# Rows of six tiles turned by VectorE in blocks of 32, and stored by blocks, in the out stage of a hybrid decoder layer

## The chip, the core and the metric

The kernel runs on one core of one Trainium2 chip. The metric is the device time of one execution in microseconds (us). The names of the engines are those of the profile: PE is TensorE (matrix products, and turns, which are products with an identity matrix), DVE is VectorE, ACT is ScalarE, POOL is GpSimd, and SP is the queue that issues nearly all DMAs.

## The reference, cut to what matters

One decoder layer on 2048 prompt tokens and 64 sample tokens, all in float32, width 1024:

```python
proj = einsum('btd,de->bte', rms_norm(x, g_mix_pre), w_in)
attn, gla_out = window_attention(proj), gated_linear_attention(proj)
mix = einsum('bte,ed->btd', concatenate([attn, gla_out], -1), w_out)
x = x + rms_norm(mix, g_mix_post)
h = rms_norm(x, g_ffn_pre)
u = relu(einsum('btd,df->btf', h, w_up))
f = einsum('btf,fd->btd', u * u, w_down)
return x + rms_norm(f, g_ffn_post), ...
```

The change lies between `mix` and `u`: the rows of `h` have to be turned, so that the 1024 columns lie along the partitions, before the product with `w_up` can be made.

## The kernel before

The tokens are 16 tiles of 128 prompt rows (0 to 15) and one tile of 64 sample rows (16). Each float32 product is made from parts: an operand is rounded to a high part (by ACT) and the rest, its low part (by DVE), and PE multiplies high by high, high by low and low by high.

**Stages.** The input projection and the attention of both kinds come first, then the out stage (about 635 to 849 us), then the up and down products in two halves of 1024 tokens each. In the first stages the code's order is kept by force on every engine (`InOrder`); tables like `G_FIRST_FILL` say how many steps of other work go between the steps of a tile. That table is for tile 0, whose queries are weighted with the decays into `XQ` by small DVE products, while PE makes the projection of the sample rows (`gproj`), which ACT and DVE fold from two halves of 64 rows into `gp_s`. In the out stage most instructions go to the engines directly (`nc.tensor`, `nc.vector`, `nc.scalar`), and the framework's scheduler sets each engine's order from the data dependencies, its own costs and the order of the code.

**The out stage.** It takes the tiles in the order `B_ORDER` = 0, 4, 1, 5, 2, 6, 3, 7, 16, 8, 12, 9, 13, 10, 14, 11, 15. Per tile i:

- The mixed operand `mt_i` is loaded (L1534) and parted: ACT makes the high part (L231), DVE the low part (L232), each in two instructions of 128x512. Two buffers alternate. Tile 15 has only half of it here.
- PE makes `out_i_0` and `out_i_1`, two halves of 512 columns in two banks, with 48 matmuls (L1581). Three in a row are high by high, high by low and low by high, so the third is the first to read the low part. Two pairs of banks alternate between the tiles.
- ACT squares both halves (L1696); DVE adds the sums (L1697), and prepares the root (L219) that POOL takes (L221). DVE weights both halves with it into `x1_i` (L1703), which frees the banks, and adds the residual in `bx_i` (L1704), stored as `x1_d`.
- ACT squares `bx_i` (L1809), then follow L219, POOL's root and the second norm into `x1_i` (L1812).
- PE turns `x1_i` with eight 128x128 products (L1822) into `xnT_i_0` and `xnT_i_1`; ACT copies these into `ht` (L1831).

The code has the norms of a tile two tiles behind its product (`early`). The tiles of a half are taken in pairs j and j + 4 (8 and 12, 9 and 13, ...). `ht` holds seven planes of 4 x 128 tokens for the pair: planes 0 and 1 are the first tile's, 6 and 2 the second's, and four subtractions (L1840) make the others for a product scheme with seven in place of eight multiplications. For tiles 8 to 15 one buffer, `ht_8`, serves all pairs. The planes are stored in `h_d`, two by L1836 after the first tile of a pair and five by L1845 after the second, and the up products fetch them later (L1857, `fetch_h`) and part them (L1899 on ACT, L1900 on DVE, called from `load_h`). `uX` is the first of the up products, `sam` the sample's, and `xsT` the turned sample rows. Tile 11's copies and the last store wait for the up stage (`late_copies`, L2153). L143 is the line of the queue that keeps an order by hand; all that passes through it bears this line.

Of the kernel before, what the change touches and what calls it, by code (L numbers as in the profile page):

```python
# [12 lines left out]
F32 = mybir.dt.float32  # L13
# [3 lines left out]
ALU = mybir.AluOpType  # L17
# [57 lines left out]
G_ORDER = (0, 1, 2, 3)  # L75
G_FILL = (3, 5, 6, 10, 8, 2, 14, 4, 4, 10, 8, 20)
G_LAST_FILL = (2, 4, 5, 7, 6, 2, 11, 2, 3, 7, 6, 15)
G_FIRST_FILL = (6, 6, 6, 10, 10, 4, 16, 4, 4, 5, 5, 20)
S_WAIT = (2, 6)
WO_PARTS = ((), (0, 1, 2), (3, 4, 5), (6, 7))  # L80
B_ORDER = (*(j + b for j in range(4) for b in (0, 4)), NB, *(j + b for j in range(4) for b in (8, 12)))
# [72 lines left out]
def hybrid_step_kernel(ctx: ExitStack, tc: tile.TileContext, I, O):  # L154
# [24 lines left out]
    def bank(shape, kind, name):  # L179

        return ps.tile(shape, F32, tag=kind, name=name, bufs=1 if kind in "de" else 2)
# [9 lines left out]
    dpool = ctx.enter_context(tc.tile_pool(name="dpool", bufs=1, space=DRAM))  # L191
    mix_d = [dpool.tile([P, KT, rows(i)], F32, name=f"mix_d{i}") for i in range(NTILE)]
    xt_d = [dpool.tile([P, 2, KT, rows(i)], F32, name=f"xt_d{i}") for i in range(NTILE)]
    h_d = [dpool.tile([P, 7, KT // 2, BT], F32, name=f"h_d{sb}") for sb in range(NSB)]
    s_d = [[dpool.tile([P, 7, BT], F32, name=f"s_d{sb}_{fc}") for fc in range(NFC)] for sb in range(NSB)]
    t_d = [dpool.tile([P, 4, 512], F32, name=f"t_d{fc}") for fc in range(NFC)]
    wo_d = [dpool.tile([P, 2, D], F32, name=f"wo_d{k}") for k in range(KT - 1)]
# [1595 lines left out]

    late_copies, latest_store = [], []

    def residual(i, banks, tensor=nc.tensor, scalar=nc.scalar, vector=nc.vector):

        n = rows(i)
        x = res_x.pop(i, None) or load_x(i)[0]
        ssq = sp.tile([P, 48], F32, tag="ssq", name=f"bssq_{i}", bufs=2)  # L1800
        junk = sp.tile([P, D], mybir.dt.bfloat16, tag="junk", name=f"bjunk_{i}", bufs=1)
        x1 = R["x"].tile([P, D], F32, tag="x1", name=f"x1_{i}", bufs=2)
        if i == NB:
            banks = [folded(x1[:NS, c * 512 : (c + 1) * 512], p_) for c, p_ in enumerate(banks)]
        if banks:
            g = g_mix if tensor is nc.tensor else [gpost[:, c * 512 : (c + 1) * 512] for c in range(2)]
            yield from mixed(i, banks, x, x1, junk, ssq, g, sp, scalar, vector)
        rs = ssq[:, 3:5]
        scalar.activation(junk[:n], x[:n], AF.Square, accum_out=ssq[:n, 2:3])  # L1809
        yield  # L1810
        rsqrt_mean(sp, rs[:n, 1:2], ssq[:n, 2:3], n, D, vector=vector)
        vector.scalar_tensor_tensor(x1[:n], x[:n], rs[:n, 1:2], gpre[:n], op0=ALU.mult, op1=ALU.mult)  # L1812
        yield
        sb, j, second = i // 8, i % 4, i % 8 >= 4
        q = slice(j * P, (j + 1) * P)
        if i < NB and not second and i:
            sums[sb, j] = sums[sb, j - 1] if sb and j else ht_place(f"ht_{i}")
        for h in range(2):
            kk = slice(h * 4, h * 4 + 4)
            pt = (bank([P, 512], "ce"[h], f"xnT_{i}_{h}") if te is tensor else next_bank("cdce", f"xnT_{i}_{h}")).rearrange("p (k t) -> p k t", k=4)  # L1820
            for k in range(4):
                tensor.transpose(pt[:, k, :n], x1[:n, (h * 4 + k) * P : (h * 4 + k + 1) * P], ident[:n, :n])  # L1822
            if i == NB:
                split_copy(xsT[:, kk, :NS], xsT[:, kk, NS:], pt[:, :, :NS], vector)
                continue
            ht = sums[sb, j]
            copy = (ht[:, (6, 2)[h] if second else h], pt, AF.Copy)
            if i == B_ORDER[-2]:
                late_copies.append(copy)
            else:  # L1830
                scalar.activation(*copy)  # L1831
            if sb == 0 and not second:
                split_copy(H[h + 1][0][:, :, q], H[h + 1][1][:, :, q], pt, vector)
        if i == NB or not second:
            if i < NB and sb and i != B_ORDER[-2]:
                nc.sync.dma_start(h_d[sb][:, :2, :, q], ht[:, :2])  # L1836
            return
        yield
        for out, a, b in ((4, 6, 0), (6, 2, 6), (5, 2, 4), (3, 1, 5)):
            vector.tensor_tensor(ht[:, out], ht[:, a], ht[:, b], op=ALU.subtract)  # L1840
            if out == 6 and i == B_ORDER[-1]:
                yield
        if i == B_ORDER[-3]:
            yield
        latest_store[:] = [nc.sync.dma_start(h_d[sb][:, 2:, :, q], ht[:, 2:])]  # L1845

    h_raws = {}

    def fetch_h(sb, p, home="h"):
        h_raws[p] = []  # L1850
        for k in range(0, KT // 2, 2):
            if isinstance(home, tuple):
                pool, tag = U[home[k // 2]], "s"
            else:
                pool, tag = {"h": hs_pool, "t": keep}.get(home) or U[home], f"{home}{k // 2}"
            raw = pool.tile([P, 2, BT], F32, tag=tag, name=f"hraw_{sb}_{p}_{k}", bufs=1)
            fetched = nc.sync.dma_start(raw, h_d[sb][:, p - 1, k : k + 2])  # L1857
            h_raws[p].append(raw)
        return fetched

    def load_h(sb, p, scalar=nc.scalar, vector=nc.vector):
        h_place(sb, p)
        for n, raw in enumerate(h_raws.pop(p)):
            split_by(scalar, vector, *(t[:, 2 * n : 2 * n + 2] for t in H[p]), raw)
            yield 1.3

    def split_apart(sb, p):
# [52 lines left out]
    for n, i in enumerate(B_ORDER[2:]):  # L1920
        early.append((i, []))
        mixing = out_projecting(nc.tensor, i, early[-1][1])
        run(mixing, 24 if i == B_ORDER[-1] else 48)
        if n == 0:
            first_rows = residual(*early.pop(0))
            next(first_rows)
            second = residual(*early.pop(0))
            next(second)
            next(second)
            run(first_rows)  # L1930
        elif n == 1:
            run(second)
        if i == B_ORDER[-1]:
            waiting_rows = residual(*early.pop(0))
            run(waiting_rows, 5)
        elif n > 1:
            run(residual(*early.pop(0)))
        run(mixing)
        if n == len(B_ORDER) - 5:
            with tc.issue_after(loaded.ins):  # L1940
                first_up = load_up(0, 0)
            with tc.issue_after(first_up.ins):
                gpost = gains(I["g_mix_post"][0], 0, "gpost")
            split_up(0, 0, 0)
            split_up(0, 0, 1)
            fetch_h(0, 5)
# [201 lines left out]
    def opening(p, taken, ahead, add):  # L2148

        if p == 1:  # L2150
            for copy in late_copies:
                ac.activation(*copy)
            nc.sync.dma_start(h_d[1][:, :2, :, 3 * P :], sums[1, 3][:, :2])  # L2153
            taken(p)
            next(last_rows)
            loaded = placing[0]
            for n, raw in enumerate(h_raws[3]):
                with tc.issue_after(loaded.ins):
                    loaded = nc.sync.dma_start(raw, h_d[0][:, 2, 2 * n : 2 * n + 2])
            next(seventh)  # L2160
        elif p == 0:
            next(last_rows)
            sums_24(0, 0, dv)
        elif p == 2:
            taken(p)
            ahead("a")
        elif p == 8:
            taken(p)
            split_sums(0, 0, 24, ac, dv)
            run(load_h(0, 6, ac, dv))  # L2170
            U.pop("tmp").release()
        elif p == 5:
            taken(p)
            next(last_rows)
            next(last_rows)
            close_pools(R)
            for q in H_LATE[3:]:
                h_pools[q] = open_pool(f"h_{q}")
            ahead("s13")
            run(load_h(0, 3, ac, dv))  # L2180
            h_place(0, 4)
            loaded = None
            for k in range(0, KT // 2, 2):
                with tc.issue_after(loaded.ins) if loaded else nullcontext():
                    loaded = nc.sync.dma_start(f32(H[4][1][:, k : k + 2]), h_d[0][:, 3, k : k + 2])
            with tc.issue_after(loaded.ins):
                latest_store[:] = [load_up(0, 2)]
        elif p == 7:
            taken(p)
            split_in_place(4)  # L2190
        elif p == 9:
            taken(p)
            ahead("13")
            ahead("s24")
            run(last_rows)
        elif p == 6:
            next_X.append(bank([P, BT], "a", "uX_0_1"))
            up_product(0, 1, 1, next_X[0])
        elif p == 3:
            with tc.issue_after(latest_store[0].ins):  # L2200
                for half in range(2):
                    load_down(0, half)
        else:
            ahead("24")
            split_up(0, 1, 1, ac, None)
            taken(6)
            add(6, 1, "Z")
            split_low(0, 1, 1, dv)
            add(1, 1, "V")
# [420 lines left out]
```

## Time and profile before

| | |
|---|---|
| runs | 2138.22, 2137.28, 2135.93 us; median 2137.28 |
| profiled execution | 2138.09 us, span 2136.3 us |
| granted PE clock | 0.999 |
| busy | PE 99%, PE's weight loads 86%, DVE 72%, ACT 57%, POOL 10% of the span |
| out stage, PE | 48 matmuls of a tile from 777.82 to 788.84 us, the turn of a tile from 777.03 to 777.82 |

A timeline row begins with the start and the duration in us, then engine, line, operation, what it writes and reads, shapes and the count of equal instructions in a row; a bracket at the end gives the idle time before it and what ended it. The duration of a row reaches to the end of its last instruction, so rows of one engine can overlap by the depth of its pipeline; the distance between starts is what an instruction costs its engine.

### The profile page before, as it was taken

Reading aid. Unit: us, or ns where it says so; the run is one execution under the profiler, and the core shown is the slowest. Engines: PE = TensorE matmul, PEld = TensorE weight load, DVE = VectorE, ACT = ScalarE, POOL = GpSimd, SP = SyncE. Lnnn points to the kernel's source line nnn. Section 1 sums busy time; section 2 is a strip of 40 time slices with the busy share of each in tenths; the row PEclk is TensorE's granted clock in tenths of the full one; section 3 lists DMA queues with packets and bytes.
Section 4 is the critical chain, followed back from the end, with each engine's and each line's share of the span. In section 5 each row is a group of like instructions: output and inputs, shape, how many; then the busy total and the mean of one; then the engine's idle time right before and its main releaser. Section 6 shows DMA issues by size and latency. Waiting matters only on the chain.

```text
span 2136.3 us, 34547 instructions
## 1 busy us (share of the span) xinstructions
PE 2124.3 (99%) x11828; PEld 1839.5 (86%) x11828; DVE 1528.0 (72%) x3209; ACT 1209.9 (57%) x2690; POOL 223.0 (10%) x393
## 2 busy tenths in 40 slices
PE   9999999999999999999999999999999999999998
PEld 9999999999998888888888888888888888888887
DVE  7999878788886667888887655557766666555576
ACT  7999867566764445655554644344454444544454
POOL 4676510000001110000000000000000000000000
PEclk9999999999999999999999999999999999999999
DMA  7444334546667668687876777668544443766685
GB/s 244 150 148 142 113 100 93 128 113 166 189 201 265 202 208 269 223 274 260 277 257 230 262 236 223 209 197 281 185 149 158 157 158 134 253 204 197 190 273 179
DMA packets 309324, 421.73 MB, mean 197 GB/s; under 512 B 80204, under 2 KB 213308, under 8 KB 305036
## 3 DMA queue, kind: packets, MB, share of 16 engines
q1 hardware_dynamic: 308988, 419.26, 61.2%
q8 instruction: 93, 1.52, 0.3%
q14 instruction: 83, 0.68, 0.1%
q10 hardware_dynamic: 160, 0.27, 0.0%
HBM read 270.34 MB, written 148.57 MB: 196 GB/s over the span
## 4 chain that ended last, share of the span: by engine, by line
PE 95%; ACT 2%; DVE 2%; DMA 1%; issue 0%; POOL 0%; DVEq 0%; SPq 0%; ACTq 0%; POOLq 0%
PE dn L143 28%; PE gproj L143 12%; PE uc L143 8%; PE uX L143 8%; PE out L1581 7%; PE proj L143 6%; PE ud L143 4%; PE ue L143 4%; PE ub L143 4%; PE sam L143 2%; PE dsam L143 1%; PE sc L143 1%; PE pT L143 1%; PE av L143 1%; PE out L143 1%; PE xT L143 1%
## 5 line engine op out<-in xcount | busy, mean ns | idle before, releaser
L143 PE MATMUL dn<-o0t,o0s 128*128 128x512 f32 x888 | 345.5, 389 | 0.5 <-DVE f L2268 0.3
L143 PE MATMUL dn<-o0t,o1s 128*128 128x512 f32 x888 | 345.6, 389 | 0.0
L143 PE MATMUL dn<-o1t,o0s 128*128 128x512 f32 x888 | 345.6, 389 | 0.0
L2254 DVE TENSOR_TENSOR o1s<-rs,o0s 128x512 fp32r<-128x512 f32 x224 | 154.7, 691 | 223.3 <-ACT o0s L2253 221.0
L2253 ACT ACTIVATE o0s<-rs 128x512 fp32r<-128x512 f32 x224 | 141.1, 631 | 295.0 <-PE dn L143 261.5
L143 PE MATMUL gproj<-wg,gxh 128*128 128x384 f32 x1024 | 269.7, 341 | 0.0
L143 ACT ACTIVATE st<-st 128x512 f32<-128x512 f32 x224 | 141.1, 630 | 103.9 <-DVE st L143 99.0
L143 PEld LDWEIGHTS dn<-o0t,o0s 128*128 128x128 f32 x888 | 166.8, 188 | 37.2 <-DVE f L2268 1.1
L143 PEld LDWEIGHTS dn<-o1t,o0s 128*128 128x128 f32 x888 | 166.7, 188 | 35.1
L143 PEld LDWEIGHTS dn<-o0t,o1s 128*128 128x128 f32 x888 | 166.7, 188 | 35.0
L143 PE MATMUL gproj<-wg,gxl 128*128 128x384 f32 x576 | 186.4, 341 | 1.7 <-DVE gp_s L143 1.6
L143 PE MATMUL uc<-H,s 128*128 128x512 f32 x768 | 186.5, 391 | 0.0
L143 PEld LDWEIGHTS gproj<-wg,gxh 128*128 128x128 f32 x1024 | 184.3, 188 | 2.5 <-issue 2.1
L143 PE MATMUL uX<-H,w 128*128 128x512 f32 x768 | 185.2, 390 | 0.0
L143 PEld LDWEIGHTS uX<-H,w 128*128 128x128 f32 x768 | 144.0, 188 | 30.3
L143 PEld LDWEIGHTS uc<-H,s 128*128 128x128 f32 x768 | 143.0, 188 | 30.6 <-ACT st L143 0.2
L1581 PE MATMUL out<-wo,mt 128*128 128x512 f32 x680 | 158.8, 392 | 0.4 <-DVE x L1703 0.3
L2254 DVE TENSOR_TENSOR o1t<-rt,o0t 128x512 fp32r<-128x512 f32 x222 | 152.2, 686 | 4.2 <-ACT o0t L2253 4.1
L1581 PEld LDWEIGHTS out<-wo,mt 128*128 128x128 f32 x680 | 126.4, 188 | 27.0 <-issue 1.0
L2253 ACT ACTIVATE o0t<-rt 128x512 fp32r<-128x512 f32 x222 | 136.9, 618 | 9.0 <-DMA rt<-t_d 7.1
L221 POOL TENSOR_TENSOR frs<-rs_v,half 128x1 f32<-128x1 f32 (+1 forms) x13 | 11.5, 891 | 1197.8 <-DVE rs_v L219 1197.8
L143 DVE TENSOR_TENSOR st<-st 128x512 f32<-128x512 f32 x160 | 110.6, 691 | 29.5 <-ACT st L143 25.2
(451 smaller groups left out, 4238.8 us busy)
## 6 DMA issues: line engine op xcount, KB each, us to landing
s_d<-st SPq DMA_DIRECT2D x32, 1792.0 KB
rs<-s_d SPq DMA_DIRECT2D x224, 256.0 KB
raw<-in_w_up SPq DMA_DIRECT2D x64, 512.0 KB
rt<-t_d SPq DMA_DIRECT2D x128, 256.0 KB
rt<-in_w_down SPq DMA_DIRECT2D x96, 256.0 KB
t<-in_w_down SPq DMA_DIRECT2D x64, 256.0 KB
t_d<-t SPq DMA_DIRECT2D x32, 512.0 KB
h_d<-ht SPq DMA_DIRECT2D x8, 1280.0 KB
```

The lines of the kernel that those rows point to most:

```text
L143: ins = call(*a, **k)
L221: return nc.gpsimd.tensor_tensor(out, v[:n], e, op=ALU.pow)
L1581: te.matmul(banks[c], x, w[:, c * 512 : (c + 1) * 512], start=k + u == 0, stop=k == KT - 1 and u == n - 1,)
L2253: high = nc.scalar.activation(hi, raw, AF.Copy)
L2254: low = nc.vector.tensor_tensor(lo, raw, f32(hi), op=ALU.subtract)
```

## The change

Four parts. First, for the tiles 8, 12, 9, 13, 10 and 14 PE's turns and ACT's copies give way to two DVE transposes of 128x512 each, which turn every 32x32 block within itself; what the whole turn would do beyond that, moving blocks between groups of 32 partitions, is left to the stores. Tiles 11 and 15 keep PE's turns, and ACT's copies write the same layout by blocks. Second, `h_d[1]` is laid out by tile, block and plane; where one DMA of 128 partitions stored, four DMAs of 32 partitions do (`store_blocks`), the subtractions work on views of 128x4x128, the fetch has runs of 128 numbers, and ACT and DVE part it through a view. Third, two numbers of `G_FIRST_FILL` change, 10, 10 to 13, 7. Fourth, `run(first_rows)` is called four matmuls into the next tile.

```diff
-G_FIRST_FILL = (6, 6, 6, 10, 10, 4, 16, 4, 4, 5, 5, 20)
+G_FIRST_FILL = (6, 6, 6, 13, 7, 4, 16, 4, 4, 5, 5, 20)
...
-    h_d = [dpool.tile([P, 7, KT // 2, BT], F32, name=f"h_d{sb}") for sb in range(NSB)]
+    h_d = [dpool.tile(s, F32, name=f"h_d{sb}") for sb, s in enumerate(([P, 7, KT // 2, BT], [P, 4, 4, 7, P]))]
...
+    def by_blocks(ht):
+        return ht.rearrange("p u k t -> p (u k t)").rearrange("p (b u k x) -> p b u k x", b=4, u=7, k=4)
+
+    def store_blocks(j, us):
+
+        ht, dst = by_blocks(sums[1, j]), h_d[1][:, j]
+        if j == 3:
+            return nc.sync.dma_start(dst[:, :, us], ht[:, :, us].rearrange("p b u k x -> p b u (k x)"))
+        for c in range(4):
+            src = ht[c * 32 : c * 32 + 32, :, us].rearrange("t a u k x -> t a (u k x)")
+            stored = nc.sync.dma_start(dst[:, c, us].rearrange("(a t) u e -> t a (u e)", a=4), src)
+        return stored
...
+            u = (6, 2)[h] if second else h
+            if 8 <= i < NB and j < 3:
+                vector.transpose(
+                    by_blocks(sums[sb, j])[:, :, u].rearrange("t a k x -> t k a x"),
+                    x1[:, h * 512 : (h + 1) * 512].rearrange("x (k a t) -> x k a t", k=4, a=4),
+                )
+                continue
...
-            copy = (ht[:, (6, 2)[h] if second else h], pt, AF.Copy)
+            out = ht[:, u]
+            if sb:
+                out = by_blocks(ht)[:, :, u].rearrange("p c k x -> p k c x")
+                pt = pt.rearrange("p k (c x) -> p k c x", c=4)
+            copy = (out, pt, AF.Copy)
...
-                nc.sync.dma_start(h_d[sb][:, :2, :, q], ht[:, :2])
+                store_blocks(j, slice(2))
...
+        t = by_blocks(ht).rearrange("p b u k x -> p u b (k x)") if sb else ht
         for out, a, b in ((4, 6, 0), (6, 2, 6), (5, 2, 4), (3, 1, 5)):
-            vector.tensor_tensor(ht[:, out], ht[:, a], ht[:, b], op=ALU.subtract)
+            vector.tensor_tensor(t[:, out], t[:, a], t[:, b], op=ALU.subtract)
...
-        latest_store[:] = [nc.sync.dma_start(h_d[sb][:, 2:, :, q], ht[:, 2:])]
+        latest_store[:] = [store_blocks(j, slice(2, 7)) if sb else nc.sync.dma_start(h_d[0][:, 2:, :, q], ht[:, 2:])]
...
-            fetched = nc.sync.dma_start(raw, h_d[sb][:, p - 1, k : k + 2])
+            if sb:
+                raw = raw.rearrange("p b t -> p (b t)").rearrange("p (m e) -> p m e", e=P)
+            src = h_d[1][:, k : k + 2, :, p - 1].rearrange("p j c e -> p (j c) e") if sb else h_d[0][:, p - 1, k : k + 2]
+            fetched = nc.sync.dma_start(raw, src)
...
+        if n == 1:
+            run(mixing, 4)
+            run(first_rows)
         run(mixing, 24 if i == B_ORDER[-1] else 48)
...
-            run(first_rows)
```

The lines move: the second norm L1812 becomes L1825, ACT's second square L1809 becomes L1822, the subtractions L1840 become L1866, the stores L1836 and L1845 become L1806, the fetch L1857 becomes L1886, and the block transposes are L1835.

The scheduler also sets other instructions in another order. Three places are shown. The first is DVE's queue where tile 12's rows and the low part of `mt_13`, the operand of the product after next, are made. Before:

```order
L1703 SCALAR_TENSOR_TENSOR x1_12_10685<-out_12_0_10447,bssq_12_10683,wo0_3_9385 128x512
L1703 SCALAR_TENSOR_TENSOR x1_12_10685<-out_12_1_10472,bssq_12_10683,wo1_3_9386 128x512
L1704 TENSOR_TENSOR bx_12_10681<-x1_12_10685,bx_12_10681 128x1024
L232 TENSOR_TENSOR mt_13_10625<-mt_13_10625 128x512 x2
L219 TENSOR_SCALAR rs_v_10697<-bssq_12_10683 128x1
L1812 SCALAR_TENSOR_TENSOR x1_12_10685<-bx_12_10681,bssq_12_10683,gpre_9738 128x1024
L1697 TENSOR_TENSOR bssq_9_10776<-bssq_9_10776 128x1
```

After:

```order
L1703 SCALAR_TENSOR_TENSOR x1_12_10678<-out_12_0_10447,bssq_12_10676,wo0_3_9385 128x512
L1703 SCALAR_TENSOR_TENSOR x1_12_10678<-out_12_1_10472,bssq_12_10676,wo1_3_9386 128x512
L1704 TENSOR_TENSOR bx_12_10674<-x1_12_10678,bx_12_10674 128x1024
L219 TENSOR_SCALAR rs_v_10690<-bssq_12_10676 128x1
L1825 SCALAR_TENSOR_TENSOR x1_12_10678<-bx_12_10674,bssq_12_10676,gpre_9738 128x1024
L1835 STREAM_TRANSPOSE ht_8_10611<-x1_12_10678 128x4x4x32 x2
L1866 TENSOR_TENSOR ht_8_10611<-ht_8_10611 128x4x128 x4
L232 TENSOR_TENSOR mt_13_10618<-mt_13_10618 128x512 x2
L1697 TENSOR_TENSOR bssq_9_10762<-bssq_9_10762 128x1
```

The low part of `mt_13` (L232) moved from behind the residual sum (L1704) to behind the second norm, the two transposes and the four subtractions of tile 12.

The second is the end of out(13), on DVE and on ACT. The names `mt_10` and `mt_14` are the operands of the next two products. DVE before:

```order
L1704 TENSOR_TENSOR bx_9_10774<-x1_9_10778,bx_9_10774 128x1024
L232 TENSOR_TENSOR mt_10_10718<-mt_10_10718 128x512 x2
L219 TENSOR_SCALAR rs_v_10790<-bssq_9_10776 128x1
L1812 SCALAR_TENSOR_TENSOR x1_9_10778<-bx_9_10774,bssq_9_10776,gpre_9738 128x1024
L1697 TENSOR_TENSOR bssq_13_10865<-bssq_13_10865 128x1
L219 TENSOR_SCALAR rs_v_10871<-bssq_13_10865 128x1
L1703 SCALAR_TENSOR_TENSOR x1_13_10867<-out_13_0_10631,bssq_13_10865,wo0_3_9385 128x512
```

DVE after:

```order
L1835 STREAM_TRANSPOSE ht_8_10611<-x1_9_10764 128x4x4x32 x2
L1697 TENSOR_TENSOR bssq_13_10844<-bssq_13_10844 128x1
L219 TENSOR_SCALAR rs_v_10850<-bssq_13_10844 128x1
L1703 SCALAR_TENSOR_TENSOR x1_13_10846<-out_13_0_10624,bssq_13_10844,wo0_3_9385 128x512
L1703 SCALAR_TENSOR_TENSOR x1_13_10846<-out_13_1_10649,bssq_13_10844,wo1_3_9386 128x512
L232 TENSOR_TENSOR mt_10_10704<-mt_10_10704 128x512 x2
L232 TENSOR_TENSOR mt_14_10786<-mt_14_10786 128x512 x2
```

ACT before:

```order
L231 ACTIVATE mt_10_10718<-mt_10_10718 128x512 x2
L1809 ACTIVATE bjunk_9_10777,bssq_9_10776<-bx_9_10774 128x1024
L1696 ACTIVATE bjunk_13_10866,bssq_13_10865<-out_13_0_10631 128x512
L1696 ACTIVATE bjunk_13_10866,bssq_13_10865<-out_13_1_10656 128x512
L1831 ACTIVATE ht_8_10611<-xnT_12_0_10701 128x512
L1831 ACTIVATE ht_8_10611<-xnT_12_1_10707 128x512
L231 ACTIVATE mt_14_10807<-mt_14_10807 128x512 x2
```

ACT after:

```order
L1822 ACTIVATE bjunk_9_10763,bssq_9_10762<-bx_9_10760 128x1024
L1696 ACTIVATE bjunk_13_10845,bssq_13_10844<-out_13_0_10624 128x512
L1696 ACTIVATE bjunk_13_10845,bssq_13_10844<-out_13_1_10649 128x512
L231 ACTIVATE mt_10_10704<-mt_10_10704 128x512 x2
L231 ACTIVATE mt_14_10786<-mt_14_10786 128x512 x2
```

On DVE the low part of `mt_10` moved from behind tile 9's residual sum to behind tile 13's weighting of its product (L1703), and on ACT the high part from ahead of the squares of `out_13_0` and `out_13_1` (L1696) to behind them.

The third is the end of the stage. DVE, around the low part of `mt_15`, before:

```order
L1703 SCALAR_TENSOR_TENSOR x1_14_11041<-out_14_0_10813,bssq_14_11039,wo0_3_9385 128x512
L1840 TENSOR_TENSOR ht_8_10611<-ht_8_10611 128x512
L1703 SCALAR_TENSOR_TENSOR x1_14_11041<-out_14_1_10838,bssq_14_11039,wo1_3_9386 128x512
L1840 TENSOR_TENSOR ht_8_10611<-ht_8_10611 128x512 x2
L232 TENSOR_TENSOR mt_15_11007<-mt_15_11007 128x512
L1840 TENSOR_TENSOR ht_8_10611<-ht_8_10611 128x512
L1704 TENSOR_TENSOR bx_14_11037<-x1_14_11041,bx_14_11037 128x1024
```

After:

```order
L1697 TENSOR_TENSOR bssq_11_11054<-bssq_11_11054 128x1
L219 TENSOR_SCALAR rs_v_11060<-bssq_11_11054 128x1
L1703 SCALAR_TENSOR_TENSOR x1_11_11056<-out_11_0_10896,bssq_11_11054,wo0_3_9385 128x512
L1703 SCALAR_TENSOR_TENSOR x1_11_11056<-out_11_1_10921,bssq_11_11054,wo1_3_9386 128x512
L1835 STREAM_TRANSPOSE ht_8_10611<-x1_14_11006 128x4x4x32 x2
L1866 TENSOR_TENSOR ht_8_10611<-ht_8_10611 128x4x128 x4
L232 TENSOR_TENSOR mt_15_10972<-mt_15_10972 128x512
```

It moved from among the subtractions of tile 14, ahead of tile 11's rows, to behind tile 11's weighting and all of tile 14's turns and subtractions. PE before has the first up product `uX` behind the turn of tile 11, which follows `out_15`:

```order
L1581 MATMUL out_15_1_11015<-wo0_3_9385,wo1_3_9386 128x512
L1822 MATMUL xnT_11_0_11117<-ident_204,x1_11_11101 128x128 x4
L1822 MATMUL xnT_11_1_11122<-ident_204,x1_11_11101 128x128 x4
L143 MATMUL uX_0_0_11204<-H10_0_9699,w00_0_0_10906 128x512
L143 MATMUL uX_0_0_11204<-H11_0_9700,w00_0_0_10906 128x512
```

PE after has it right behind `out_11_1` (first piece), and `out_15` begins behind the first eight `sam` (second piece):

```order
L1581 MATMUL out_11_1_10921<-wo1_3_9386,mt_11_10890 128x512
L1581 MATMUL out_11_1_10921<-wo0_3_9385,mt_11_10890 128x512
L143 MATMUL uX_0_0_11162<-H10_0_9699,w00_0_0_10878 128x512
L143 MATMUL uX_0_0_11162<-H11_0_9700,w00_0_0_10878 128x512
L143 MATMUL uX_0_0_11162<-H10_0_9699,w01_0_0_10879 128x512
```

```order
L143 MATMUL sam_0_11166<-w01_0_0_10879,xsT_9724 128x256
L143 MATMUL sam_0_11166<-w00_0_0_10878,xsT_9724 128x256
L143 MATMUL sam_0_11166<-w01_0_0_10879,xsT_9724 128x256
L1581 MATMUL out_15_0_10976<-wo0_1_9218,mt_15_10972 128x512
L1581 MATMUL out_15_0_10976<-wo1_1_9219,mt_15_10972 128x512
L1581 MATMUL out_15_0_10976<-wo0_1_9218,mt_15_10972 128x512
```

So 12 `uX` and 8 `sam` matmuls moved from behind out(15) to ahead of it.

On SP the four stores of tile 8's planes come ahead of the load of `mt_13`, and those of tile 12 ahead of the load of `mt_10`.

More of the change, by code (lines that the diff above doesn't have):

```diff
@@ L1835, in residual @@
             if i < NB and sb and i != B_ORDER[-2]:
-                nc.sync.dma_start(h_d[sb][:, :2, :, q], ht[:, :2])
+                store_blocks(j, slice(2))
             return
         yield
+        ht = sums[sb, j]
+        t = by_blocks(ht).rearrange("p b u k x -> p u b (k x)") if sb else ht
         for out, a, b in ((4, 6, 0), (6, 2, 6), (5, 2, 4), (3, 1, 5)):
-            vector.tensor_tensor(ht[:, out], ht[:, a], ht[:, b], op=ALU.subtract)
+            vector.tensor_tensor(t[:, out], t[:, a], t[:, b], op=ALU.subtract)
             if out == 6 and i == B_ORDER[-1]:
@@ L1863, in load_h @@
         for n, raw in enumerate(h_raws.pop(p)):
-            split_by(scalar, vector, *(t[:, 2 * n : 2 * n + 2] for t in H[p]), raw)
+            parts = [t[:, 2 * n : 2 * n + 2] for t in H[p]]
+            if sb:
+                parts = [t[:, :, n * 256 : n * 256 + 256].rearrange("p k (m x) -> p m k x", x=32) for t in H[p]]
+                raw = raw.rearrange("p m (k x) -> p m k x", k=4)
+            split_by(scalar, vector, *parts, raw)
             yield 1.3
@@ L2152, in opening @@
                 ac.activation(*copy)
-            nc.sync.dma_start(h_d[1][:, :2, :, 3 * P :], sums[1, 3][:, :2])
+            store_blocks(3, slice(2))
             taken(p)
```

## The prediction

> **What bounds the kernel now.** I read the shares of busy time, the chain that ended last and TensorE's waits, and then the timeline of the out stage engine by engine.
>
> ```profile
> span 2136.3 us, 34547 instructions
> PE 2124.3 (99%) x11828; PEld 1839.5 (86%) x11828; DVE 1528.0 (72%) x3209; ACT 1209.9 (57%) x2690; POOL 223.0 (10%) x393
> PE 95%; ACT 2%; DVE 2%; DMA 1%; issue 0%; POOL 0%; DVEq 0%; SPq 0%; ACTq 0%; POOLq 0%
> PE gproj L143 <- DVE gp_s L143: 1.6, 1, 1.6
> PE out L1581 <- DVE x L1703: 0.3, 1, 0.3
> ```
>
> TensorE (PE) is busy for 99% of the span and carries 95% of the chain; its longest wait on another engine here is 1.6 us, the one in the sample's projection. So whatever PE no longer executes shortens the kernel by as much, and whatever makes PE wait lengthens it by as much. VectorE (DVE) is busy 72% overall, but the question is its lateness in this one stage.
>
> ```profile
> 766.01 11.18 PE L1581 MATMUL out<-wo,mt 128*128 128x512 f32 x48
> 777.03 1.03 PE L1822 MATMUL xnT<-ident,x 128*128 128x128 f32 x8
> 777.82 11.18 PE L1581 MATMUL out<-wo,mt 128*128 128x512 f32 x48
> 788.84 1.03 PE L1822 MATMUL xnT<-ident,x 128*128 128x128 f32 x8
> ```
>
> These are out(9), the turn of tile 8, out(13), the turn of tile 12. PE never stops. A turn costs 777.82 - 777.03 = 0.79 us, a product 788.84 - 777.82 = 11.02, so 0.23 per matmul. The third matmul of a product is the first that reads the low part of its operand mt, 0.46 after it begins.
>
> **What the change takes away.** Six turns leave PE: 6 x 0.79 = 4.74 us. Their twelve ScalarE (ACT) copies go too, but ACT is off the path.
>
> ```profile
> 319.21 0.58 ACT L143 ACTIVATE gp_s<-gproj,rstd_all 64x384 f32<-64x384 f32 x1
> 319.68 2.10 DVE L143 TENSOR_TENSOR XQ<-dec,qz 128x256 f32<-128x256 f32 x6
> 321.69 0.61 DVE L143 SCALAR_TENSOR_TENSOR gp_s<-gproj,rstd_all,gp_s 64x384 f32<-64x384 f32 x1
> 322.36 5.82 PE L143 MATMUL gproj<-wg,gxl 128*128 128x384 f32 x32 [1.60 <-DVE gp_s L143]
> ```
>
> The weighted queries: ACT's half of the folding is done at 319.8, but DVE folds only at 321.69, behind six products, and PE waits 1.60 (since 320.76). With the folding first it is done at 319.8 + 0.61 = 320.4, before PE asks: -1.6. The six products then end 0.6 later, in a row that now stands idle for PE's sake; nothing in the trace waits on them soon enough, so 0. The later turn of the first rows changes no engine's order (only names differ), so 0. Gains together: 6.34 us.
>
> **What it adds, on DVE's queue.** Twelve block turns of 128x512:
>
> ```profile
> L143 DVE STREAM_TRANSPOSE blocks<-gp 128x512 f32<-128x512 f32 x14 | 9.9, 704 | 0.0
> ```
>
> The row has 0.70 us each; back to back I take 0.62, as equal 128x512 work is spaced 0.60 (791.52 to 792.12, below) for 0.69 listed. Strided views could make it dearer; 0.62 to 0.70 moves each stall below by under 0.2. By itself this is 8 us of DVE time and harmless; what matters is where it stands. In the order, tile 13's low part (L232) is no longer right behind the residual sum of tile 12, but behind its norm, its two turns and its four subtractions; 10's and 15's likewise stand behind the work of the tile before. I walk DVE's new order with old durations.
>
> ```profile
> 762.12 0.37 SPq L1845 DMA_DIRECT2D h_d<-ht  x1
> 768.13 0.32 SPq L1857 DMA_DIRECT2D hraw<-h_d  x1
> 763.16 1.22 DVE L1704 TENSOR_TENSOR bx<-x,bx 128x1024 f32<-128x1024 f32 x1
> 766.47 1.29 DVE L1812 SCALAR_TENSOR_TENSOR x<-bx,bssq,gpre 128x1024 f32<-128x1024 f32 x1 [0.66 <-POOL bssq L221]
> 767.67 0.15 DVE L1697 TENSOR_TENSOR bssq<-bssq 128x1 f32<-128x1 f32 x1
> 768.76 1.41 DVE L1703 SCALAR_TENSOR_TENSOR x<-out,bssq,wo 128x512 f32<-128x512 f32 x2
> 770.20 1.23 DVE L1704 TENSOR_TENSOR bx<-x,bx 128x1024 f32<-128x1024 f32 x1
> 774.17 1.16 ACT L231 ACTIVATE mt<-mt 128x512 fp32r<-128x512 f32 x2 [6.64 <-DMA mt<-mix_d]
> 774.83 1.29 DVE L232 TENSOR_TENSOR mt<-mt 128x512 fp32r<-128x512 f32 x2 [3.40 <-ACT mt L231]
> ```
>
> *Stall 1, out(13).* Before, the low part of mt_13 began at 774.83, in good time. After, tile 8's turns follow its norm (ended 767.67) and need the buffer of turned rows, whose store (762.12) is read back from 768.13: they run 768.1 to 769.35. From L1697 to L1704 it is 770.20 - 767.67 = 2.53, so tile 12's L1704 starts at 771.9. From a tile's L1704 to the end of its norm is 767.67 - 763.16 = 4.51 (ACT's squares and GpSimd's root lie between): 776.4. Two turns: 777.65; four subtractions at 0.605: 780.07; the first low part 0.69: 780.76. PE, with no turn of tile 8, wants it at 777.03 + 0.46 = 777.49. Stall 3.3. (Its high part: the load now queues on SP behind four block stores, lands about 776.7 by the 5.6 us from issue at 768.55 to 774.17, and is under this stall.)
>
> ```profile
> 768.55 0.40 SPq L1534 DMA_DIRECT2D mt<-mix_d  x1
> 789.04 0.60 ACT L1696 ACTIVATE bjunk<-out 128x512 bf16<-128x512 f32 x1 [1.39 <-PE out L1581]
> 789.76 0.16 DVE L1697 TENSOR_TENSOR bssq<-bssq 128x1 f32<-128x1 f32 x1 [0.76 <-ACT bjunk L1696]
> 790.85 0.75 DVE L1703 SCALAR_TENSOR_TENSOR x<-out,bssq,wo 128x512 f32<-128x512 f32 x1 [0.74 <-POOL bssq L221]
> 791.52 0.68 DVE L1840 TENSOR_TENSOR ht<-ht 128x512 f32<-128x512 f32 x1
> 792.12 0.74 DVE L1703 SCALAR_TENSOR_TENSOR x<-out,bssq,wo 128x512 f32<-128x512 f32 x1
> 792.78 1.28 DVE L1840 TENSOR_TENSOR ht<-ht 128x512 f32<-128x512 f32 x2
> ```
>
> *Stall 2, out(10).* Now ACT squares out(13) before it rounds mt_10, and DVE does tile 13's L1697 and both L1703 before mt_10's low part. All of these need the end of out(13), T, which is also when PE wants mt_10. Before, T was 788.84, the square came at 789.04, L1697 at 789.76, L1703 at 790.85 = T + 2.01. Two L1703 take 0.67 + 0.66; the low part 0.69: T + 4.03. PE wants it at T + 0.46: stall 3.6. It doesn't depend on how late anything else is.
>
> *out(14) and out(11).* T is now 777.03 + 11.02 + 3.3 = 791.4; mt_14's low part follows mt_10's by about 7 us at most (its load waits for out(13) to end), PE wants it 14.6 later. mt_11's, behind tile 13's turns and three subtractions in the order, has a margin of some 4 us by the same walk. No stall.
>
> ```profile
> 836.99 1.03 PE L1822 MATMUL xnT<-ident,x 128*128 128x128 f32 x8
> 837.78 3.02 PE L143 MATMUL uX<-H,w 128*128 128x512 f32 x12
> 841.59 2.93 PE L143 MATMUL uX<-H,w 128*128 128x512 f32 x12
> 845.31 2.92 PE L143 MATMUL uc<-H,s 128*128 128x512 f32 x12
> 848.07 1.03 PE L143 MATMUL xnT<-ident,x 128*128 128x128 f32 x8
> 840.34 1.41 DVE L143 SCALAR_TENSOR_TENSOR x<-out,bssq,gpost 128x512 f32<-128x512 f32 x2 [0.74 <-POOL bssq L221]
> 847.21 0.69 DVE L143 TENSOR_TENSOR t<-t,raw 128x512 f32<-128x512 f32 x1
> ```
>
> *Stall 3, out(15).* The first 12 uX and 8 sample matmuls (845.31 - 841.59 = 3.72) move in front of out(15). They write a bank that out(11) held, free after its L1703: T + 2.01 + 0.67 = T + 2.7 of idling, T now being out(11)'s end. They end at T + 6.4, PE wants mt_15's low part at T + 6.9. DVE delivers it behind L1703 twice, two turns, four subtractions: T + 2.01 + 1.33 + 1.25 + 2.42 + 0.69 = T + 7.7. Idle 2.7 + 0.8 = 3.5.
>
> *Stall 4, turn of tile 15.* Before, PE came at 848.07 for rows whose norm was over by DVE's next row, 847.21: 0.86 in hand. PE now comes 3.72 sooner after out(15), DVE's L1703 sooner by 1.35 (840.34 was 3.35 after out(15)'s end at 836.99, kept by other DVE work; 2.0 now, as at 790.85): 0.86 - 3.72 + 1.35 = -1.5. Stall 1.5.
>
> **Sum.** -4.74 - 1.6 + 3.3 + 3.6 + 3.5 + 1.5 = +5.6 on the profiled execution, which took 2138.09, 0.8 above the runs' median of 2137.28 and inside their range. So 2143.7 by it, 2142.9 by the median; I say 2143.3, between them. Bounds: were stalls 1, 3 and 4 nothing, 6.3 - 3.6 = -2.7 (2134.6); with late stores, below, +5 more.
>
> **Stores and fetches.** SP issues 18 more DMAs here:
>
> ```profile
> 440.59 1.76 SPq L143 DMA_DIRECT2D qk_d<-blocks  x4
> 1246.53 1.06 ACT L1899 ACTIVATE H<-hraw 128x1024 fp32r<-128x1024 f32 x1 [3.19 <-DMA hraw<-h_d]
> ```
>
> Four take 1.76, so 18 x 0.44 = 7.9 us of a queue with gaps of many us; counted above where mt_13's load stands behind four, else 0. One whole store landed within 768.13 - 762.12 = 6.0 us. If four 32-partition pieces take the same, tile 9's turn (about 787.7) finds tile 12's store (issued from 780.1) gone; I take 6.0, the nearest row; the ends are 3 (four pieces side by side, with longer runs of bytes) and 12 (pieces two by two, each pair as long as the whole). [...] The fetch of turned rows in 512-byte runs has its first use at 1246.53, where ACT already waits; before PE asks there are a few us, so 0.
>
> **Rivals.**
> B, faster: DVE keeps up and only the gains remain, 2138.1 - 6.3 = 2131.8. For it: DVE idles 3.40 before 774.83, so there is room. Against: that idling lies ahead of a low part which now stands behind seven more instructions. It decides at mt_13's low part done by 777.5, and at ACT rounding mt_10 before out(13) ends; the latter the order excludes.
> C, no change: stall 2 stays, the others shrink to about 3 together as ACT, GpSimd and DVE answer sooner with fewer copies queued: 2138.1 - 6.3 + 3.6 + 3 = 2138.4, range 2135 to 2141.
> D, slower still: pieces land in 12 us. Tile 9's turn then waits until 792, tile 13's L1697 behind it; tile 10's and 14's in the same way. Tile 9's turns are free until 791.0 (1.25 before tile 13's L1697, which can start at 791.4 + 0.9), 10.9 after the store; tile 10's by the same walk until 7.6 after tile 13's store. Beyond that each us late holds back the next low part by one: 1.1 and 4.4, so 2143.3 + 5.5 = 2149. [...]
> E, slower: the fetches in 512-byte runs (4 KB before) come late in the down products, four of them by 1 us beyond what PE has in hand: 2147.
>
> **Chances.** A (2141.6 to 2146.5) 0.58, D 0.12, E 0.05, C 0.17, B 0.08. This kernel's runs spread 0.1%, so 0.2% (4.3 us: 2133.0 to 2141.6) is about what can be told from none. Faster 0.08 is B, same 0.17 is C, slower 0.75 is A, D and E. The range leaves out B and the upper part of D: 2136 to 2149.
>
> **What will show it.** PE waiting at the third matmul of out(13) for DVE mt for 3 us; at the first or third of out(10) for 3.6; at uX ahead of out(15) for DVE x for 2.7, and at xnT of tile 15 for x; 48 xnT gone; the gp_s wait gone; block turns near 0.7 us each. I am wrong if DVE's turns wait for DMA by more than 1 us at tiles 9, 13, 10 or 14 (D), if they cost over 1 us (each stall grows by 0.6 or more), or if PE doesn't wait at out(10), where my argument is strongest.

## The result: slower, by more than was forecast

The changed kernel takes 2151.49 us (median, 2151.12 to 2152.59), the kernel before 2137.75 in the runs beside it: 1.0066 times as long, 95% interval 1.0049 to 1.0084. That is +13.7 us where +5.6 was forecast. The profiled execution took 2151.56 us, its span is 2149.8. Two of the runs below, pin_all and lay, have one execution that took far longer than their others (3012 and 5477 us); it is left out of their times.

The first lines of the page after (span; busy time, share and instructions of each engine):

```profile
span 2149.8 us, 34455 instructions
PE 2125.3 (99%) x11780; PEld 1837.8 (85%) x11780; DVE 1535.3 (71%) x3221; ACT 1203.6 (56%) x2678; POOL 224.2 (10%) x393
```

PE executes 48 instructions fewer than before and yet is busy 1.0 us longer. So the 4.7 us of turns are gone, and something else makes PE's remaining instructions longer by about as much and more. The waits of PE on other engines, engine and line, then the total in us, the count and the longest:

```profile
PE out L1581 <- DVE mt L232: 4.6, 2, 2.8
PE uX L143 <- ACT st L143: 3.3, 1, 3.3
PE uX L143 <- DVE x L1703: 2.7, 1, 2.7
PE out L1581 <- ACT mt L231: 1.7, 2, 1.3
PE gproj L143 <- DVE gp_s L143: 0.2, 1, 0.2
```

The first four are new, 12.2 us together; the last is the fold, 1.6 before. PE's timeline shows where they lie (start, duration, instruction, and in the bracket the idle time before it):

```profile
764.91 11.18 PE L1581 MATMUL out<-wo,mt 128*128 128x512 f32 x48
776.45 0.73 PE L1581 MATMUL out<-wo,mt 128*128 128x512 f32 x2 [0.36 <-ACT mt L231]
779.93 12.06 PE L1581 MATMUL out<-wo,mt 128*128 128x512 f32 x46 [2.75 <-DVE mt L232]
793.29 0.73 PE L1581 MATMUL out<-wo,mt 128*128 128x512 f32 x2 [1.30 <-ACT mt L231]
795.90 34.09 PE L1581 MATMUL out<-wo,mt 128*128 128x512 f32 x142 [1.88 <-DVE mt L232]
832.65 4.36 PE L143 MATMUL uX<-H,w 128*128 128x512 f32 x12 [2.66 <-DVE x L1703]
853.25 4.46 PE L143 MATMUL uX<-H,w 128*128 128x512 f32 x12 [3.25 <-ACT st L143]
862.18 3.02 PE L143 MATMUL ud<-H,s 128*128 128x512 f32 x12
```

The turns of tiles 8 to 14 are gone from it. out(13) stops at its third matmul, out(10) at its first and third, the first uX (now ahead of out(15)) and the second uX wait too. And each time what follows is slow: 46 matmuls of out(13) take 12.06 us, where 46 x 0.23 + 0.16 = 10.7 was due; 12 uX take 4.36 and 4.46, where they took 3.02 and 2.93 before. The granted clock (fourth column; the rest are the stretch's length, PE's busy time and count, the DMA share and GB/s) says why. The stretches are cut where the clock changes, with the 3.41 us ahead of each change:

```profile
core 0: us, PE busy (x), PEclk, DMA share, GB/s
775.98:779.39 3.41, 0.84 (x3) 1.00 0.32 129
779.39:782.81 3.42, 2.88 (x7) 0.50 0.74 158
793.05:796.46 3.41, 1.30 (x4) 1.00 0.95 327
796.46:799.87 3.41, 3.41 (x9) 0.50 0.77 311
```

From 779.39 to 782.81 PE is granted half its clock: 3.4 us, 2.88 of them busy, and the 46 matmuls take 1.4 us longer. The same happens behind the waits at out(10), from 796.46, and behind those at the two uX, from 834.01 and 854.49.

The account, on PE from out(12) to ud, which began at 848.86 before and at 862.18 now, +13.3: gains upstream 1.1, turns 4.74; waits 0.36 + 2.75 + 1.30 + 1.88 + 2.66 + 3.25 = 12.2; slow matmuls 1.45 (out(13)) + 1.44 (out(10)) + 1.56 (uX and sam) + 1.67 (uX and sam) = 6.1. -1.1 - 4.74 + 12.2 + 6.1 = 12.5. The 0.8 left fits the way idle time is counted: from a row's modelled end, which lies 0.16 past the spacing of the starts (11.18 against 11.02 for a product), so six waits are up to 1.0 longer than their idle times say. Behind ud the two kernels run alike: the spans differ by 13.5.

### The profile page after: what moved, and what is told of

It reads as the page before. It is cut to its first block, busy times and chain, and to the rows that moved or that the text cites. A ratio compares the mean times of both kernels' runs of the same rounds, so it can differ in the third digit from the quotient of the medians.

```text
span 2149.8 us, 34455 instructions
## 1 busy us (share of the span) xinstructions
PE 2125.3 (99%) x11780; PEld 1837.8 (85%) x11780; DVE 1535.3 (71%) x3221; ACT 1203.6 (56%) x2678; POOL 224.2 (10%) x393
## 4 chain that ended last, share of the span: by engine, by line
PE 62%; DVE 1%; DMA 1%; ACT 0%; issue 0%; POOL 0%; DVEq 0%; ACTq 0%
PE dn L143 27%; PE uX L143 8%; PE uc L143 8%; PE ud L143 4%; PE ue L143 4%; PE ub L143 4%; PE out L1581 3%; PE sam L143 2%; PE dsam L143 1%; DMA rs<-s_d 1%; DMA hraw<-h_d 0%; DVE o1s L2289 0%; DVE o1t L2289 0%; PE ua L143 0%; DVE f L2303 0%
## 5 line engine op out<-in xcount | busy, mean ns | idle before, releaser
L143 PEld LDWEIGHTS uc<-H,s 128*128 128x128 f32 x768 | 143.0, 188 | 30.3
```

Of the source, the lines that this page charges most:

```text
L143: ins = call(*a, **k)
```

## Experiments

Two theories stood against each other at first. O: the loss is the order that the scheduler now chooses (waits) and, C, a lower clock behind each long wait. W and S: DVE's added work, or the stores by 32 partitions, cost by themselves. Ratios are to the kernel before, run on the same chip.

### small: the two small parts alone

```diff
-G_FIRST_FILL = (6, 6, 6, 10, 10, 4, 16, 4, 4, 5, 5, 20)
+G_FIRST_FILL = (6, 6, 6, 13, 7, 4, 16, 4, 4, 5, 5, 20)
...
+        if n == 1:
+            run(mixing, 4)
+            run(first_rows)
```

> The kernel before with only two of the change's four parts: the two numbers of G_FIRST_FILL, and the first rows' turn four matmuls later. All theories: the wait of PE for the fold gp_s (1.6 us before) shrinks to 0.2, so 1.2 to 1.6 us less, 2136.2 by the median; no change of order in the out stage, and no wait there. If these parts carried any of the loss, the time would be above 2138.

2136.35 us against 2138.5, ratio 0.9991 (0.9982 to 0.9999). A small gain, in the direction and of the size expected, at the edge of what the runs can tell; its profile has the wait for gp_s at 0.2 us. These two parts carry none of the loss.

### pin_all: operands put back by pins

```diff
+        if i in PINNED:
+            high, low = mixed_by[B_ORDER[B_ORDER.index(i) + 2]]
+            tc.add_manual_dep(square.ins, high.ins.name, ahead, reason="operand first")
+            tc.add_manual_dep(normed.ins, low.ins.name, ahead, reason="operand first")
...
+    te.last = last_out[0].ins.name
```

A part of the edit that isn't shown puts the stores by blocks behind the load of the next operand in SP's order; the last line shown puts uX behind out(15).

> The changed kernel, with the low and high parts of mt_13, mt_10, mt_14, mt_11 and mt_15 put back where they stood on DVE and ACT before, their loads ahead of the block stores, and uX behind out(15). Theory O (the loss is the scheduler's new order: 12.2 us of PE waits in four places, and some 6.2 us of slow matmuls behind them at a granted clock of 0.50): both go, 2151.5 - 18.4 = 2133, below the kernel before; no wait over 1 us between out(9) and the up products. Rival W (the blocks' work on DVE and the 24 small stores themselves are too much at this place): waits move elsewhere, time at or above 2143.

2152.09 us, ratio 1.0065 (1.0052 to 1.0078): the number is that of rival W, and theory O as I had put it missed by 19 us. PE's timeline says more than the number:

```profile
762.76 43.82 PE L1587 MATMUL out<-wo,mt 128*128 128x512 f32 x192
812.54 18.66 PE L1587 MATMUL out<-wo,mt 128*128 128x512 f32 x72 [5.96 <-DVE x L1709]
```

DVE's timeline, at mt_15's low part and at the residual rows of tile 15:

```profile
811.04 0.69 DVE L1560 TENSOR_TENSOR mt<-mt 128x512 fp32r<-128x512 f32 x1 [6.16 <-ACT mt L1559]
854.20 1.23 DVE L144 TENSOR_TENSOR bx<-x,bx 128x1024 f32<-128x1024 f32 x1 [9.93 <-DMA bx<-in_x_prompt]
```

Four products, out(9) to out(14), run as 192 matmuls without a pause, all six turns' time gained. But the scheduler answered the pins with two new misplacements: mt_15's low part now stood on DVE ahead of tile 10's weighting and waited 6.16 us for its high part, and the residual rows of tile 15 were loaded behind the four stores of tile 14 on SP, 9.93 us. PE waited 5.96 us at out(11) for the first and 7.18 at the turn of tile 15 for the second. So W isn't shown by it either: the waits are again of order, at other places. This run settled only that these single pins don't remove the loss.

### lay: the block layout without DVE's turns

The branch with `vector.transpose` is taken out, so PE turns all tiles; the whole turns are then stored where turned blocks are expected, so the prompt's rows reach the up products rearranged (the work is the same).

> The changed kernel with PE's turns kept for all tiles, ACT copying into the block layout; stores of four DMAs, fetch by blocks, and the two small parts stay. Theory O: DVE's and PE's order are nearly those of before, so the time is that of the small parts, 2136 to 2138. Rival S (the 32-partition stores or the fetch in 512-byte runs cost): above 2141, with waits on DMA in the out stage or at the down products from 1240 us.

2154.5 us, ratio 1.0075 (1.0062 to 1.0088). It has no DVE turn, and is slower still, so theory O's 2136 to 2138 missed: the order didn't stay that of before. PE waits once at the place, 14.78 us, at out(11). The timeline's rows of SP's queue and of ACT:

```profile
793.53 25.03 SPq L1806 DMA_DIRECT2D h_d<-ht  x12
825.08 1.15 ACT L231 ACTIVATE mt<-mt 128x512 fp32r<-128x512 f32 x2 [9.37 <-DMA mt<-mix_d]
```

Here the scheduler put twelve block stores in a row on SP, 25 us from the first to the last; the last four need tile 13's subtractions, which DVE ended at 815.02, and the load of mt_11, issued at 818.66, stands behind them. Rival S is right that the stores can cost, but here mainly by their place in SP's order: the load was held behind stores whose rows weren't made. DVE's turns are not needed for a loss.

### idle: waits put into the kernel before

```diff
+IDLE = {2: 4, 3: 5, 8: 6, 9: 8, 14: 3}
...
+                for _ in range(0 if k else IDLE.get(i, 0)):
+                    nc.vector.tensor_tensor(
+                        lo.rearrange("p h t -> p (h t)"), before_banks[0][1], g_mix[0], op=ALU.add
+                    )
```

> The kernel before with added DVE instructions ahead of the low parts of mt_2, mt_3, mt_8, mt_9 and mt_14 (4, 5, 6, 8 and 3 of them, each about 0.6 us, begun when the product before has ended), so that PE waits there by 1 to 4 us, each time after a long busy stretch. Theory C (a wait that is long enough also halves the granted clock for about 3.4 us): the waits under about 1.7 us leave the clock at 1.00, those of 2.7 us and more show some 3.4 us at 0.50 and cost about 1.5 us on top, so the time is the sum of the waits plus 3 to 5 us over before (about 2137 + 10 + 4). Rival (a wait costs its length, the slow matmuls of the changed kernel have another cause, such as its DMA or DVE traffic): clock 1.00 throughout, 2137 + 10.

2168.81 us, in two executions: 30.3 more than the 2138.50 of the kernel before. The waits came out longer than planned, 7.58, 4.22, 4.17, 6.68 and 0.27 (23 us), as other DVE work went ahead of the added; so the threshold between 1.7 and 2.7 wasn't tried here. The clock behind the first of them, which ended at 694.42:

```profile
core 0: us, PE busy (x), PEclk, DMA share, GB/s
690.00:692.00 2.00, 0.00 (x0) 0.76 0.95 324
692.00:694.00 2.00, 0.00 (x0) 0.50 0.06 25
694.00:696.00 2.00, 1.58 (x4) 0.50 0.57 173
696.00:698.00 2.00, 2.00 (x7) 0.53 0.96 290
698.00:700.00 2.00, 2.00 (x10) 1.00 0.96 246
```

In the kernel before, whose clock is 1.00 up to its last 5 us, a wait alone brings the half clock; here it falls 4 us after the wait began and returns 3.4 us after work resumed. 44 matmuls took 11.89 there, 10.3 was due. C holds for long waits: the 23 us of waiting cost 30, where the rival had them cost their length.

### paced: the whole order of the place by hand

All instructions of tiles 8 to 15 on DVE, ACT and SP are chained in a written order, and uX goes behind out(15); its core:

```diff
+                vector += [("res", i), ("norm", i)]
+                scalar += [("sq", i, 0), ("sq", i, 1), ("sq2", i)]
...
+                    scalar += [("hi", after, k) for k in (0, 4) if ("hi", after, k) in marks]
+                    vector += [("lo", after, k) for k in (0, 4) if ("lo", after, k) in marks]
+                    vector += [("turn", i, h) for h in range(2)]
...
+            queue.append(("x1", i))
...
+                queue += [("load", B_ORDER[m + 3])] + [("store", i, c) for c in range(4)]
```

> The changed kernel with the out stage's order written out by hand for tiles 8 to 15: on DVE each low part of mt right behind the second norm and ahead of the turns and subtractions, tile 8's turns behind tile 12's weighting; on ACT the second square ahead of the high part; on SP each load of mt and bx ahead of the four block stores that it stood behind; uX behind out(15). Theory O (the loss is the order alone; pin_all failed because its pins left other loads and low parts behind): no PE wait over 1 us from out(9) to the end of the first up products, clock 1.00, and the six turns' 4.7 us and the fold's 1.3 us come through: 2131 to 2133, 4 us below the run small. Rival W (DVE's and SP's added work doesn't fit here in any order): at least one wait of over 2 us remains and the time is above 2137.

2134.24 us against 2138.05, ratio 0.9979 (0.9971 to 0.9988): 17 us less than the changed kernel, with the same instructions, and below the kernel before. Its waits of PE at the place are all below 1 us (total, count, longest), and the clock stays at 1.00:

```profile
PE out L1582 <- ACT mt L1555: 0.9, 1, 0.9
PE out L1582 <- DVE mt L1556: 0.9, 1, 0.9
PE uX L143 <- ACT st L143: 0.8, 1, 0.8
```

O is shown: the work fits, the order was the loss. It misses 2131 to 2133 by 1.2 us, less than these three, 2.6 together.

### late10 and late13: one misplacement each put back

late10 chains mt_10's high part behind `("sq", 13, 1)` and its low part behind `("w", 13, 1)`; late13 chains mt_13's low part behind the subtractions of tile 12.

> paced with one misplacement of the changed kernel put back: mt_10's high part behind ACT's squares of out(13), its low part behind DVE's weighting of out(13). Theory C (a wait of 3.2 us also brings 3.4 us at half clock): PE waits 3.2 us in two pieces at out(10) as in the changed kernel, and the time is paced + 4.6. Rival (a wait costs its length): paced + 3.2. Rival W: no clear difference, as the time is lost elsewhere.

> paced with the low part of mt_13 behind tile 12's subtractions, as in the changed kernel. Walked with paced's order: PE waits 2 to 3 us at the third matmul of out(13). Theory C: paced + the wait + 1.4 to 1.7. Rival (length alone): paced + the wait. If the wait is under 1.6 us, no drop of the clock is expected.

late10: 2138.06 us, +3.8 on paced, its interval 0.9990 to 1.0009. PE's timeline there:

```profile
775.41 11.45 PE L1582 MATMUL out<-wo,mt 128*128 128x512 f32 x48 [1.61 <-ACT mt L1555]
788.15 1.20 PE L1582 MATMUL out<-wo,mt 128*128 128x512 f32 x4 [1.29 <-ACT mt L1555]
791.95 39.11 PE L1582 MATMUL out<-wo,mt 128*128 128x512 f32 x164 [2.60 <-DVE mt L1556]
```

and the granted clock (fourth column) around the first and the last of these waits:

```profile
772.26:775.67 3.41, 1.80 (x8) 1.00 1.02 391
775.67:779.08 3.41, 3.41 (x15) 1.00 0.30 89
789.33:792.74 3.41, 0.81 (x4) 1.00 0.38 100
792.74:796.15 3.41, 3.41 (x9) 0.50 0.94 328
```

The wait at out(10) is 3.9 in two pieces, and the clock falls behind it; 164 matmuls take 1.3 more than 164 x 0.23. The wait of 1.61 at out(13), which stands alone, left the clock at 1.00, like the 1.60 of the kernel before. PE waits 5.5 in all at the place, 2.6 in paced; 2.9 and the 1.3 of slow matmuls are 4.2, near the 3.8 measured. That number lies between C's forecast of 4.6 and the rival's of 3.2 and doesn't decide by itself; the clock does. late13: its profiled execution waits 1.83 and 0.88 us at out(13), the clock falls to 0.50 behind them, and the span is 1.9 us longer; but the median, 2134.32, is paced's within 0.1. By the runs it is undecided. The waits of the place only moved, 2.7 us in all against paced's 2.6, so a difference could come from the clock alone.

### warm: the changed kernel with its waits filled

```diff
+EXTRA, PRE, EARLY, LATE = {13: ((1, 10),), 10: ((1, 7),)}, {10: 5}, 10, 12
...
+                        more = te.matmul(spare[0], wo[0][0][:, :P], wo[0][0][:, :512], start=True, stop=True)
```

> The changed kernel, its order on DVE, ACT and SP kept by hand, with spare matmuls of 128x512 into an unused bank where PE waited: 10 ahead of the third matmul of out(13), 5 ahead of the first and 7 ahead of the third of out(10), 10 ahead of the first uX and 12 ahead of the second uX. Each is 0.23 us, so they fill the waits (10.1 of 12.2 us) without lengthening them. Theory C (after a wait of over about 2.7 us in a stretch of 3 the granted clock falls to half for some 3.4 us): clock 1.00 all through and about 6 us less than the changed kernel, 2145 to 2146. Rival (the slow matmuls come with the DMA and DVE traffic of that place, not with the waits): clock as in the changed kernel, time 2151 or more.

2144.81 us, ratio 1.0036 (1.0022 to 1.0050): 6.7 less than the changed kernel, with 44 matmuls more; C had said 2145 to 2146. The clock by stretches, here and in the changed kernel:

```profile
core 0: us, PE busy (x), PEclk, DMA share, GB/s
776.00:784.00 8.00, 8.00 (x35) 1.00 0.77 170
850.00:860.00 10.00, 10.00 (x54) 1.00 1.03 388
```

```profile
core 0: us, PE busy (x), PEclk, DMA share, GB/s
776.00:784.00 8.00, 4.88 (x15) 0.79 0.59 156
850.00:860.00 10.00, 6.75 (x26) 0.83 0.99 348
```

Same order, same places, a DMA share no lower: the idling itself brought the half clock, and it was worth 6 to 7 us of the 13.7.

### paced2: a better version

On SP the load of mt_13 goes ahead of a fetch and of bx_9; on DVE tile 12's turns ahead of mt_13's low part; mt_10's parts ahead of tile 9's second square and norm.

> paced with the load of mt_13 ahead of the fetch and bx_9 on SP, tile 12's turns ahead of mt_13's low part (DVE idled 2.2 us there), and mt_10's parts ahead of tile 9's second square and norm. Theory O: the waits of 0.94 at out(13) and 0.91 at out(10) go, 1.5 to 2 us less than paced: 2132.5. If DVE is at its limit here the waits come back at out(11) and the time is that of paced.

2130.71 us against 2137.9, ratio 0.9966 (0.9954 to 0.9979): 7.2 us below the kernel before. That it is also 1.8 below the forecast isn't explained. out(9) to the half of out(15) is one stretch without a pause; one wait is left at the place, at the second uX, by PE's timeline:

```profile
762.87 60.65 PE L1582 MATMUL out<-wo,mt 128*128 128x512 f32 x264
834.92 3.02 PE L143 MATMUL uX<-H,w 128*128 128x512 f32 x12 [1.38 <-ACT st L143]
```

## Why the prediction was right and wrong

**Right: the direction, three of the four waits' places, and, in part by luck, their sum.** Rival B (the freed time comes through) failed at its own condition: mt_13's low part was done at 779.9, not 777.5. The timeline of after on DVE (the subtractions of tile 12's folding, then the low parts of mt_13 and mt_10) and on ACT (the copies before the second uX):

```profile
776.57 2.70 DVE L1866 TENSOR_TENSOR ht<-ht 128x512 f32<-128x512 f32 x4
779.19 1.28 DVE L232 TENSOR_TENSOR mt<-mt 128x512 fp32r<-128x512 f32 x2
795.16 2.55 DVE L232 TENSOR_TENSOR mt<-mt 128x512 fp32r<-128x512 f32 x4
851.64 1.07 ACT L143 ACTIVATE ht<-xnT 128x512 f32<-128x512 f32 x2
852.59 0.60 ACT L143 ACTIVATE st<-uX 128x512 f32<-128x512 f32 x1
```

and all the block turns as one group (busy us, mean ns of one, idle before them):

```profile
L1835 DVE STREAM_TRANSPOSE ht<-x 128x512 f32<-128x512 f32 x12 | 7.8, 690 | 0.5 <-DMA h_d<-ht 0.5
```

- Gains. Six turns: 4.74, as said. The fold: 1.6 forecast, 1.1 to 1.4 found (0.2 of the wait is left).
- Block turns: 0.69 us each with strided views, as taken.
- Stall 1: 3.3 forecast, 0.36 + 2.75 = 3.1 found. The low part began at 779.19 against 780.07 by the walk.
- Stall 2: 3.6 forecast, 1.30 + 1.88 = 3.2 found, for the reason given (squares, weighting, then the low part at 795.16).
- Stall 3: 2.7 + 0.8 forecast; 2.66 found, and no wait behind it: the low part of mt_15 was done at 837.7, and PE, held up by 1.56 us of slow uX and sam, asked at 838.5. In warm, where uX ran at the full clock, PE waited 0.65 at that place.
- Stall 4: the wrong instruction. Not the turn of tile 15 waits, but the second uX, 3.25: it adds onto a bank that ACT first copies into st, and that copy (852.59) stands on ACT behind the squares of out(15), two high parts and two copies of ht. I had moved the first uX forward in the walk and hadn't asked what the second one, now close behind out(15), waits for.

The four come to 11.9 forecast and 12.2 found. That they agree so well is luck: stall 3 came out 0.8 smaller, and stall 4 was 1.75 larger and at another instruction. Rival C (stalls 1, 3 and 4 shrink to about 3 together) didn't come about: they are 9.0.

**Wrong: the term that wasn't there.** The step that failed is the rule on which the sum is built, "whatever makes PE wait lengthens it by as much". At four places PE's waiting cost its length and then about 1.5 us more: 6.1 us of slow matmuls, shown apart by warm (6.7). With it the sum is 5.6 + 6.1 + 0.8 that the rows' ends hide + 0.3 for the waits' sizes + 0.5 for the fold = 13.3. The kernel before couldn't show it at these places, since its only longer wait, 1.60, leaves the clock at 1.00; the profile's row of granted clock is flat there, and a flat row is no evidence of what a new wait would do.

Behind each of the four the clock stayed at 0.50 for 3.4 us. What brought it there wasn't the length of a single wait: a wait of 2.66 us, and pairs of 1.83 and 0.88 (late13) or 1.30 and 1.88, sufficed, where single waits of 1.60 (the kernel before) and 1.61 (late10) didn't; the last section shows what told them apart.

**Rival D** (stores land in 12 us) didn't come about: tile 9's turn ran at 787.55 without a wait, behind stores issued from 779.30, so those took at most 8.3. No run shows the 12 us, which were my estimate, twice the 6.0 of a whole store; whether a single piece is slower wasn't measured. **Rival E**: ACT waits 3.50 us for the first fetch in place of 3.19, and PE doesn't (ACT's timeline of after):

```profile
1259.78 1.06 ACT L1932 ACTIVATE H<-hraw 128x1024 fp32r<-128x1024 f32 x1 [3.50 <-DMA hraw<-h_d]
```

## What to carry to other kernels

When work moves from a full engine to one with room, read the new order, not the new busy time: the gain was there (paced2 has it), and a scheduler's order turned it into four waits and 13.7 us. Price a wait of PE at its length plus what the clock loses behind it: here 1.3 to 1.7 us more (the changed kernel and late10) wherever 2.06 us or more of one 3.41 us step were idle, by one wait or by two. On SP, where in lay a load behind twelve stores kept PE waiting for 14.78 us, loads that the bound engine needs go ahead of stores that nobody awaits; and single pins moved the trouble here, while a whole written order removed it.

## What the hardware showed that was not expected

In these traces the granted clock falls by time windows, not at the wait: behind the 2.66 us before the first uX it was still 1.00 for 1.3 us of work, then 0.50 for 3.4. In each trace the changes of the clock lie on one grid of 3.413 us: the four drops of the changed kernel are 5, 11 and 6 steps apart, the first two of idle (691.04 and 725.18) 10. Counted on that grid, PE was idle for 2.57, 2.11, 2.06 and 2.18 us of the steps ahead of these drops, for 2.60 in late10 and 2.21 in late13. A step at full clock with 1.90 (in idle, from 786.62) or less was followed by no drop in any trace. A single wait of 2.06 us, at a down product in the profiled execution of small (2139.90 us, the longest of its eleven), fell into one step, and that was enough (columns as above):

```profile
1473.62:1477.03 3.41, 1.34 (x6) 1.00 0.82 276
1477.03:1480.45 3.42, 3.42 (x9) 0.50 0.64 180
```

So by these traces what counts is how much of one step is idle, with the limit between 1.90 and 2.06 us, and a wait divided between two steps can be longer and leave the clock alone. Where the grid lies against the kernel differs between the traces; whether that makes the executions of late13 differ isn't shown, since only one of them has a profile.

Spare matmuls in the waits (44 in warm) kept the clock at 1.00, and the time came down all the same. Four stores of five planes took SP 3.50 us (from 779.30), where four of two planes took 1.82 (from 768.33). That isn't a price by size: the first two of both groups took 0.32 and 0.42 us alike, the third and fourth 0.46 and 0.47 with two planes and 1.00 and 1.61 with five; what held those up isn't shown.
